# Every second chunk of the up-projections by seven products of halves, and the gated products by way of DRAM

## The chip, the cores and the metric

The kernel runs on one core of one Trainium2 chip. The time is the device time of one launch in microseconds (us), the median of several runs. The engines of the core run side by side, each through its own list of instructions in order, and wait for each other by semaphores: TensorE (PE in the profile, its weight loads PEld), VectorE (DVE), ScalarE (ACT), GpSimd (POOL) and the queue that issues the transfers (SP). TensorE writes its results into eight banks of accumulator memory (PSUM), each 128 partitions by 512 float32; all other tiles lie in on-chip memory (SBUF), 128 partitions wide.

## The reference

A trunk of two decoder layers over a residual stream of 512 tokens by 1024 features, float32. Layer 0 mixes by dilated banded attention, layer 1 by forgetting attention over shared keys and values; after each mixer stands a gated ConvFFN, and it is the ConvFFN that the change touches:

```python
def conv_ffn(xn, w_up, cw, cb, w_down):
    a = xn @ w_up                                   # (512, 1024) @ (1024, 5632)
    T = a.shape[1]
    ap = jnp.pad(a, ((0, 0), (CONV_W - 1, 0), (0, 0)))
    a = sum(ap[:, j:j + T] * cw[j] for j in range(CONV_W)) + cb
    gate, val = jnp.split(a, 2, axis=-1)            # 2816 gates, 2816 values
    return (jax.nn.gelu(gate, approximate=True) * val) @ w_down
```

After it the result is normed and added to the stream. Between the two layers a shared key, value and forget-gate projection is computed from the stream.

## The kernel before

**Products.** Every float32 operand is kept as two tiles, a rounded high part (type fp32r) and the rest. `mm3` (L228) makes one float32 product of three matmuls: high by high (L229), high by low (L230), low by high (L231).

**Weights.** All weight matrices are one list of pieces in the order of use. `Weights` loads a piece (one slab, 128 x 1024 float32, 512 KB; L41, on SP's queue, into a tile `wraw` of the pool t4), `high` rounds it on ScalarE (L49), `low` subtracts on VectorE (L55), and both go into one tile `w` of the pool t8. `get` (L64) hands out the next piece and first splits pieces until `ahead - 1` more are ready; loads go `ahead_dma` pieces further. The order of all instructions on every engine is that of the program text: nothing is reordered, and an instruction that waits holds up all behind it on its engine.

**The ConvFFN** (`ffn`, L497). The activations stand transposed as `bd.xT`: four tiles of the pool t8 (two high, two low), each 128 features by 4 groups by 512 tokens. The 2816 gates and values are 22 chunks of 128 each. For chunk c a product of 24 matmuls with 512 columns gives the gates in one bank, and another the values (`up`; `feat_mm`, L307); the first two chunks are computed in halves of 256 tokens (`first_products`, L465) because the last token blocks arrive late. After the products of chunk c comes `post(c)`: per bank one ACTIVATE on ScalarE (L517, middle tap and bias), two instructions on VectorE (L518, L520, the other taps), then the GELU on ScalarE (L522) and the gated product on GpSimd (L525), which is kept in six tiles `hT` of the pool t8. The down-projection (`Proj`, L315) takes the 22 pieces of `w_down` as moving operands and the gated products, split in pairs of chunks by `prep` (L505 ScalarE, L506 VectorE), as weights, into eight banks `acc`. Its last four pieces are worked block by block, and `Boundary` norms each block (L236 to L283) and transposes it for the next stage.

**After the first ConvFFN** four token blocks of shared values are computed from four pieces (`values`, from L905). Blocks 2 and 3 are transposed in the middle of that (`bd2.transpose`), and `W.ahead` there is 4, and 3 from the transpose of block 2 on (L921).

**Pools.** t8 has 17 tiles of 8 KB a partition, t4 9 of 4 KB, t2 6 of 2 KB; a tile handed out again waits until its last user is done.

## Time and profile before

| | |
|---|---|
| median of 3 runs | 1169.48 us (1168.93 to 1169.65) |
| the profiled execution | 1168.88 us, span 1167.1 us |
| TensorE busy | 1153.6 us, 99% of the span |
| VectorE, ScalarE, GpSimd busy | 57%, 44%, 17% |
| the two stretches of `up` products (chunks 2 to 21 of a layer) | 217.6 and 217.7 us |
| transfers | 115.72 MB, mean 99 GB/s |

The span is what lies between the first and the last instruction of the profiled execution; its own time lies 1.8 us above it. A row of the timeline gives start, duration, engine, line, operation, the tile written and the tiles read, and in brackets how long the engine stood idle before and what released it. Matmuls are pipelined: a row's duration overlaps the next matmul, so the pace is read from the starts. "x2" in a row says that two instructions in a row were merged; the duration is that from the start of the first to the end of the last.

### The profile page before, as it was taken

What the parts mean: (1) busy time and instruction counts of PE and PEld (TensorE: products, weight loads), DVE (VectorE), ACT (ScalarE), POOL (GpSimd) and SP (SyncE); (2) the same over time, 40 slices, a digit from 0 to 9 for tenths busy, and PEclk for the clock granted to TensorE, in tenths of its full rate; (3) what the DMA queues carried; (4) which work ended last, traced back from release to release, by engine and by line L of the source; (5) the groups of instructions that cost most, each with busy time, mean ns of one, the idle gap of its engine ahead of it and who ended that gap; (6) DMA issues with size and microseconds to landing.
All of it is one profiled execution on the core that took longest, in us unless ns stands there. A gap on an engine that the chain in (4) does not pass through costs nothing.

```text
span 1167.1 us, 15131 instructions
## 1 busy us (share of the span) xinstructions
PE 1153.6 (99%) x5898; PEld 960.1 (82%) x5898; DVE 663.8 (57%) x991; ACT 515.8 (44%) x900; POOL 203.9 (17%) x231
## 2 busy tenths in 40 slices
PE   9999999999999999999999999999999999999997
PEld 6888889888888888888778888789888888888886
DVE  6433586655655674406464788757566566575304
ACT  5444665333433463306462677755433334354202
POOL 2722000212212210000000565400122122120000
PEclk9999999999999999999999999999999999999999
DMA  8131063333333355203204344264332332244001
GB/s 294 53 110 37 3 182 109 103 97 108 90 91 108 93 167 169 60 1 85 81 1 128 100 119 126 76 201 126 91 109 83 99 108 88 93 145 162 1 1 72
DMA packets 134849, 115.72 MB, mean 99 GB/s; under 512 B 5753, under 2 KB 119913, under 8 KB 134778
## 3 DMA queue, kind: packets, MB, share of 16 engines
q1 hardware_dynamic: 133498, 110.57, 31.0%
q0 software_dynamic: 1280, 4.20, 1.5%
q8 instruction: 46, 0.75, 0.3%
q14 instruction: 25, 0.20, 0.1%
HBM read 108.41 MB, written 2.15 MB: 95 GB/s over the span
## 4 chain that ended last, share of the span: by engine, by line
PE 89%; DVE 5%; ACT 3%; issue 2%; DVEq 0%; ACTq 0%
PE up L231 12%; PE up L229 12%; PE up L230 12%; PE acc L229 9%; PE acc L230 9%; PE acc L231 9%; PE v_ps L229 2%; PE v_ps L231 2%; PE v_ps L230 2%; PE qk_ps L230 2%; PE qk_ps L229 2%; PE qk_ps L231 2%; PE first L229 1%; PE first L230 1%; PE first L231 1%
## 5 line engine op out<-in xcount | busy, mean ns | idle before, releaser
L55 DVE TENSOR_TENSOR w<-wraw,w 128x1024 fp32r<-128x1024 f32 x182 | 262.3, 1467 | 93.5 <-ACT w L49 93.0
L49 ACT CAST w<-wraw 128x1024 fp32r<-128x1024 f32 x182 | 184.9, 1048 | 61.6 <-PE acc L231 38.3
L517 ACT ACTIVATE bb<-up,conv 128x512 f32<-128x512 f32 x80 | 62.4, 780 | 272.8 <-PE up L231 272.8
L525 POOL TENSOR_TENSOR hT<-bb 128x512 f32<-128x512 f32 x44 | 92.8, 2108 | 490.8 <-DVE bb L520 348.9
L518 DVE SCALAR_TENSOR_TENSOR bb<-up,conv,bb 128x511 f32<-128x511 f32 x80 | 60.0, 749 | 173.0 <-ACT bb L517 173.0
L229 PE MATMUL acc<-w,hs 128*128 128x512 f32 (+1 forms) x356 | 138.0, 388 | 1.1 <-DVE mix L276 1.1
L230 PE MATMUL acc<-w,hs 128*128 128x512 f32 (+1 forms) x356 | 137.8, 387 | 0.0
L231 PE MATMUL acc<-w,hs 128*128 128x512 f32 (+1 forms) x356 | 137.8, 387 | 0.0
L229 PE MATMUL up<-xbh,w 128*128 128x512 f32 x320 | 124.6, 389 | 0.0
L230 PE MATMUL up<-xcl,w 128*128 128x512 f32 x320 | 124.6, 389 | 0.0
L231 PE MATMUL up<-xbh,w 128*128 128x512 f32 x320 | 124.6, 389 | 0.0
L230 PE MATMUL up<-xbl,w 128*128 128x512 f32 x320 | 124.6, 389 | 0.0
L229 PE MATMUL up<-xch,w 128*128 128x512 f32 x320 | 124.6, 389 | 0.0
L231 PE MATMUL up<-xch,w 128*128 128x512 f32 x320 | 124.6, 389 | 0.0
L229 PEld LDWEIGHTS acc<-w,hs 128*128 128x128 f32 x356 | 66.9, 188 | 14.9 <-DVE mix L276 1.3
L231 PEld LDWEIGHTS acc<-w,hs 128*128 128x128 f32 x356 | 66.9, 188 | 13.5
L230 PEld LDWEIGHTS acc<-w,hs 128*128 128x128 f32 x356 | 66.9, 188 | 13.5
L231 PEld LDWEIGHTS up<-xch,w 128*128 128x128 f32 x320 | 60.1, 188 | 12.6
L229 PEld LDWEIGHTS up<-xbh,w 128*128 128x128 f32 x320 | 60.1, 188 | 12.5
L230 PEld LDWEIGHTS up<-xbl,w 128*128 128x128 f32 x320 | 60.1, 188 | 12.5
L230 PEld LDWEIGHTS up<-xcl,w 128*128 128x128 f32 x320 | 60.1, 188 | 12.5
L231 PEld LDWEIGHTS up<-xbh,w 128*128 128x128 f32 x320 | 60.1, 188 | 12.3
(241 smaller groups left out, 2085.7 us busy)
## 6 DMA issues: line engine op xcount, KB each, us to landing
wraw<-in_w_up_dram SPq DMA_DIRECT2D x88, 512.0 KB
wraw<-in_w_down_dram SPq DMA_DIRECT2D x44, 512.0 KB
wraw<-in_w_kvf_dram SPq DMA_DIRECT2D x16, 512.0 KB
wraw<-in_w_qkv_a_dram SPq DMA_DIRECT2D x16, 256.0 KB
wraw<-in_w_q_b_dram SPq DMA_DIRECT2D x8, 512.0 KB
ck<-cd SPq DMA_DIRECT2D x8, 512.0 KB
qst<-qst POOLq DMA_DIRECT2D x16, 256.0 KB, 3.5
wraw<-in_w_o_b_dram SPq DMA_DIRECT2D x8, 512.0 KB
```

The source lines that it names most:

```text
L49: self.nc.scalar.copy(pair[:, 0], raw)
L55: self.nc.vector.tensor_tensor(pair[:, 1], raw, pair[:, 0].bitcast(F32), ALU.subtract)
L229: pe.matmul(o, ah, bh, start=first, stop=False, skip_group_check=shared)
L230: pe.matmul(o, ah, bl, start=False, stop=False, skip_group_check=shared)
L231: pe.matmul(o, al, bh, start=False, stop=last, skip_group_check=shared)
L517: act.activation(bb[:, s, :], ps, AF.Identity, bias=cp[:, 3, ch:ch + 1], scale=cp[:, 2, ch:ch + 1])
L518: dve.scalar_tensor_tensor(bb[:, s, 1:], ps[:, :T - 1], cp[:, 1, ch:ch + 1], bb[:, s, 1:], ALU.mult, ALU.add)
L525: pool.tensor_tensor(hT[c // 4][:, c % 4, :], bb[:, 0, :], bb[:, 1, :], ALU.mult)
```

## The change

**Seven products.** For the chunks in `SEVEN` (6, 8, ... 20, eight in each layer) gates and values are taken as one product of a 2 x 2 matrix of weight halves (gates over values, first over second half of the 1024 input features) by a 2 x 2 matrix of activation halves (first over second half of the features, first and second 256 tokens). It is computed by seven products of such halves and sums in place of eight: each product is 12 matmuls with 256 columns. The sums of activations (`sums_in`: two additions on GpSimd, four subtractions on VectorE, then high and low parts in four new tiles XA and XB) are made once per layer during chunks 2 to 5. The sums of weights (`seven_weights`) are made for every such chunk two chunks ahead: four subtractions or additions of 512 columns on VectorE, and four pairs of high and low parts in place of two. The partial results are combined in the banks: a copy on ScalarE (`s1`) and five additions on VectorE, some of them between products that go on accumulating in the same bank. Between them stand the steps of the weights for chunk c + 2 and, before the last product, the first half of the gates of chunk c + 1 (`begun`).

**The chunk's end.** `post` of a chunk is put behind the first products of the next one. The gated product moves from GpSimd to VectorE, one chunk later still; it goes into a t2 tile `hc` and from there by a transfer of 256 KB to a DRAM tensor `hD`. For the down-projection `prep` reads two chunks at a time (512 KB) back into t4 tiles `hraw`. The six tiles `hT` are gone.

**Weights.** During `ffn` `W.ahead` is 1, and the steps of splitting are placed by hand between products; before the down-projection it is 4 again. In the values after the first ConvFFN it is 1 until block 3 is transposed, and then one piece is split per block.

```diff
--- before.py
+++ after.py
@@ -55,6 +55,13 @@
             self.nc.vector.tensor_tensor(pair[:, 1], raw, pair[:, 0].bitcast(F32), ALU.subtract)
             self.ready[self.n_split] = (pair[:, 0], pair[:, 1])
             self.n_split += 1
+    def take(self, k):
+        self.load(self.n_split + k + self.ahead_dma)
+        raws = [self.raw.pop(self.n_split + i) for i in range(k)]
+        self.n_split += k
+        return raws
 
     def split(self, n):
         while self.n_split < min(n, len(self.pieces)):
@@ -494,14 +501,25 @@
         dve.tensor_copy(cp, pc)
         return cp
 
+    SEVEN = range(6, NF - 1, 2)
     def ffn(bd, cp, nxt, ahead):
-        hT = [None] * 6
-        hs = {}
+        hD = tc.dram_tile([NF, 128, T], F32, name="hD")
+        hraw, hs, hc = {}, {}, {}
+        def load_h(j):
+            if j < NF // 2:
+                hraw[j] = t4([128, 2, T], name="hraw")
+                sp.dma_start(hraw[j], hD[2 * j:2 * j + 2].rearrange("c p t -> p c t"))
 
         def prep(j):
             if j < NF // 2:
+                load_h(j + 1)
                 hs[j] = t = t8([128, 2, 2, T], F32R, name="hs")
-                src = hT[j // 2][:, 2 * (j % 2):2 * (j % 2) + 2, :]
+                src = hraw.pop(j)
                 act.copy(t[:, 0], src)
                 dve.tensor_tensor(t[:, 1], src, t[:, 0].bitcast(F32), ALU.subtract)
 
@@ -510,7 +528,7 @@
                 prep(kc // 2 + 1)
             return hs[kc // 2][:, 0, kc % 2], hs[kc // 2][:, 1, kc % 2]
 
-        def post(c, banks):
+        def taps(c, banks):
             bb = t4([128, 2, T], name="bb")
             for s, ch in ((0, c), (1, NF + c)):
                 ps = banks[s]
@@ -519,25 +537,173 @@
                                          ALU.mult, ALU.add)
                 dve.scalar_tensor_tensor(bb[:, s, 2:], ps[:, :T - 2], cp[:, 0, ch:ch + 1], bb[:, s, 2:],
                                          ALU.mult, ALU.add)
+            return bb
+        gated = []
+        def product():
+            if gated:
+                c, bb = gated.pop()
+                if c - 1 in hc:
+                    sp.dma_start(hD[c - 1], hc.pop(c - 1))
+                hc[c] = t2([128, T], name="hc")
+                dve.tensor_tensor(hc[c], bb[:, 0, :], bb[:, 1, :], ALU.mult)
+        def glu(c, bb):
             act.activation(bb[:, 0, :], bb[:, 0, :], AF.Gelu_apprx_tanh)
-            if c % 4 == 0:
-                hT[c // 4] = t8([128, 4, T], name=f"hT{c // 4}")
-            pool.tensor_tensor(hT[c // 4][:, c % 4, :], bb[:, 0, :], bb[:, 1, :], ALU.mult)
-
+            gated.append((c, bb))
+        def post(c, banks):
+            product()
+            glu(c, taps(c, banks))
+        xT = None
+        XA, XB = [], []
+        def sums_in():
+            v = [t8([128, 4, T], name=f"xsum{i}") for i in range(2)]
+            for i in range(2):
+                pool.tensor_tensor(v[i], xT[0][i].bitcast(F32), xT[1][i].bitcast(F32), ALU.add)
+            yield
+            dve.tensor_tensor(v[0][:, :, LO], v[0][:, :, HI], v[0][:, :, LO], ALU.subtract)
+            dve.tensor_tensor(v[0][:, :, HI], v[1][:, :, HI], v[0][:, :, HI], ALU.subtract)
+            yield
+            dve.tensor_tensor(v[1][:, :, HI], v[1][:, :, HI], v[0][:, :, LO], ALU.subtract)
+            dve.tensor_tensor(v[1][:, :, LO], v[1][:, :, LO], v[1][:, :, HI], ALU.subtract)
+            yield
+            for X, src in ((XA, v[0]), (XB, v[1])):
+                X += [t8([128, 4, T], F32R, name="xsh"), t8([128, 4, T], F32R, name="xsl")]
+                for k in (0, 2):
+                    act.copy(X[0][:, k:k + 2], src[:, k:k + 2])
+                    dve.tensor_tensor(X[1][:, k:k + 2], src[:, k:k + 2], X[0][:, k:k + 2].bitcast(F32), ALU.subtract)
+                    yield
+        halves = {}
+        def split_pair(pair, src, n=1024):
+            act.copy(pair[:, 0, :n], src)
+            yield
+            dve.tensor_tensor(pair[:, 1, :n], src, pair[:, 0, :n].bitcast(F32), ALU.subtract)
+        def seven_weights(c):
+            r0, r1 = W.take(2)
+            w = [t8([128, 2, 1024], F32R, name="w") for _ in range(4)]
+            sa, sb = (t4([128, 1024], name="wsum") for _ in range(2))
+            a11, a12, a21, a22 = r0[:, 0:512], r0[:, 512:1024], r1[:, 0:512], r1[:, 512:1024]
+            act.copy(w[0][:, 0], r0)
+            dve.tensor_tensor(sa[:, 0:512], a11, a21, ALU.subtract)
+            dve.tensor_tensor(sb[:, 0:512], a21, a22, ALU.add)
+            yield
+            dve.tensor_tensor(sa[:, 512:1024], sb[:, 0:512], a11, ALU.subtract)
+            act.copy(w[1][:, 0], sa)
+            dve.tensor_tensor(sb[:, 512:1024], a12, sa[:, 512:1024], ALU.subtract)
+            yield
+            dve.tensor_tensor(w[1][:, 1], sa, w[1][:, 0].bitcast(F32), ALU.subtract)
+            act.copy(w[2][:, 0], sb)
+            yield
+            dve.tensor_tensor(w[0][:, 1], r0, w[0][:, 0].bitcast(F32), ALU.subtract)
+            act.copy(w[3][:, 0, 0:512], a22)
+            yield
+            dve.tensor_tensor(w[2][:, 1], sb, w[2][:, 0].bitcast(F32), ALU.subtract)
+            yield
+            dve.tensor_tensor(w[3][:, 1, 0:512], a22, w[3][:, 0, 0:512].bitcast(F32), ALU.subtract)
+            v = [t.rearrange("p s (q k c) -> p s q k c", q=2, k=4) for t in w]
+            halves[c] = dict(A11=v[0][:, :, 0], A12=v[0][:, :, 1], S3=v[1][:, :, 0], S2=v[1][:, :, 1],
+                             S1=v[2][:, :, 0], S4=v[2][:, :, 1], A22=v[3][:, :, 0])
+        def plain_weights():
+            for _ in range(2):
+                W.high()
+                W.low()
+                yield
+        def weights(c):
+            return seven_weights(c) if c in SEVEN else plain_weights()
+        def half_mm(o, w, x, s, start):
+            for k in range(4):
+                mm3(o, w[:, 0, k, :], w[:, 1, k, :], x[0][:, k, s], x[1][:, k, s], start and k == 0, k == 3, True)
+        def up(w, o, kcs):
+            wh, wl = (t.rearrange("p (k c) -> p k c", k=8) for t in w)
+            for kc in kcs:
+                bh, bl = xs(xT, kc, ALL)
+                mm3(o, wh[:, kc, :], wl[:, kc, :], bh, bl, kc == 0, kc == KD - 1)
+        base = W.n_get
         first = first_products(bd, 4)
+        xT = bd.xT
         post(0, first[0:2])
         post(1, first[2:4])
+        W.ahead = 1
+        W.split(base + 8)
+        extra = sums_in()
+        begun = None
+        before = None
         for c in range(2, NF):
+            if c == NF - 2:
+                load_h(0)
             if c == NF - 1:
                 prep(0)
                 prep(1)
-            banks = []
-            for s in range(2):
-                o = bank([128, T], name="up")
-                feat_mm(W.get(), bd.xT, o, ALL)
-                banks.append(o)
-            post(c, banks)
-
+            steps = weights(c + 2)
+            banks = [bank([128, T], name="up") for _ in range(2)]
+            if c in SEVEN:
+                w = halves.pop(c)
+                W.n_get += 2
+                x11, x21, x22 = [(xT[0][i], xT[1][i], s) for i, s in ((0, LO), (1, LO), (1, HI))]
+                o1, o2, o3, o4 = banks[0][:, LO], banks[0][:, HI], banks[1][:, LO], banks[1][:, HI]
+                s1, s12, s17 = (t2([128, 256], name="csum") for _ in range(3))
+                def prod(o, a, x, start=False):
+                    half_mm(o, w[a], x[0:2], x[2], start)
+                prod(o1, "A11", x11, True)
+                prod(o2, "S2", (*XB, HI))
+                prod(o3, "S3", (*XA, HI), True)
+                product()
+                bb = taps(*before)
+                act.copy(s1, o1)
+                next(steps)
+                dve.tensor_tensor(s12, o2, s1, ALU.add)
+                dve.tensor_tensor(s17, o3, s1, ALU.add)
+                glu(before[0], bb)
+                prod(o1, "A12", x21)
+                prod(o2, "S1", (*XA, LO))
+                prod(o3, "A22", (*XB, LO))
+                next(steps)
+                next(steps, None)
+                dve.tensor_tensor(o4, o2, s17, ALU.add)
+                begun = W.get(), bank([128, T], name="up")
+                up(*begun, range(4))
+                prod(o2, "S4", x22)
+                next(steps, None)
+                dve.tensor_tensor(o3, o3, s12, ALU.add)
+                next(steps, None)
+                dve.tensor_tensor(o2, o2, s1, ALU.add)
+            else:
+                for s in range(2):
+                    if s == 0 and begun:
+                        w, banks[0] = begun
+                        up(*begun, range(4, KD))
+                        begun = None
+                    else:
+                        up(W.get(), banks[s], range(KD))
+                    if s == 0 and before:
+                        post(*before)
+                    next(steps, None)
+                    next(extra, None)
+            for _ in steps:
+                pass
+            before = c, banks
+        post(*before)
+        product()
+        sp.dma_start(hD[NF - 1], hc.pop(NF - 1))
+        W.ahead = 4
         Proj(NF, 4, get_act).finish(nxt, ahead)
 
 
@@ -910,6 +1076,7 @@
     bd2.norm(3)
     banks = [bank([128, 512], name="v_ps") for _ in range(4)]
     wv = []
+    W.ahead = 1
     for sp_, blocks in ((0, (0, 1)), (2, (0, 1)), (0, (2,)), (2, (2,)), (0, (3,)), (2, (3,))):
         if len(wv) < 4:
             wv += [value_weight(), value_weight()]
@@ -918,9 +1085,11 @@
                 values(banks, wv[s], s, (b,))
             if (sp_, b) == (2, 0):
                 bd2.transpose(2)
-                W.ahead = 3
         if (sp_, blocks) == (0, (2,)):
             bd2.transpose(3)
+            W.ahead = 3
+        if blocks[0] > 1:
+            W.split(min(W.n_split + 1, W.n_get + W.ahead))
         if sp_ == 2 and blocks[-1] > 1:
             for bb in (blocks[0] - 2, blocks[0]):
                 keep_values(0, bb, banks[bb])
```

## The prediction

> **What bounds the kernel now.** I read the page first, then the stretches, then the starts of the matmuls, and last the rows of the other engines.
>
> ```profile
> PE 1153.6 (99%) x5898; PEld 960.1 (82%) x5898; DVE 663.8 (57%) x991; ACT 515.8 (44%) x900; POOL 203.9 (17%) x231
> PEclk9999999999999999999999999999999999999999
> PE 89%; DVE 5%; ACT 3%; issue 2%; DVEq 0%; ACTq 0%
> ```
>
> TensorE is busy throughout, at a granted clock in the top tenth, and makes up 89% of the chain that ended last. So the matmuls count, provided that no other engine becomes late. The two stretches of `up`, by the windows:
>
> ```profile
> 205.40:423.00 217.60, 217.60 (x962) 180.29 (x961) 129.73 (x122) 81.25 (x102) 42.94 (x20) 1.00 0.34 100
> 822.20:1039.90 217.70, 217.70 (x963) 180.41 (x962) 129.74 (x122) 81.22 (x102) 42.90 (x20) 1.00 0.34 100
> ```
>
> After the length stand the busy times of PE, PEld, DVE, ACT and POOL: TensorE has no gap, VectorE works 129.7 of 217.6 us. The pace is in the starts, 42 matmuls of 256 columns apart, then 45 of 512:
>
> ```profile
> 185.02 0.28 PE L231 MATMUL first<-xbh,w 128*128 128x256 f32 x1
> 190.06 0.28 PE L231 MATMUL first<-xbh,w 128*128 128x256 f32 x1
> ...
> 206.60 0.39 PE L231 MATMUL up<-xbh,w 128*128 128x512 f32 x1
> 216.80 0.39 PE L231 MATMUL up<-xbh,w 128*128 128x512 f32 x1
> ```
>
> 5.04/42 = 0.1200 us and 10.20/45 = 0.2267 us. Half the columns cost 53% of the time.
>
> **The matmuls.** A plain chunk is 48 x 0.2267 = 10.88 us; a chunk of seven products is 7 x 12 x 0.1200 = 10.08 us. That saves 0.80 us, 16 times: 12.8 us, far less than the eighth that the arithmetic saves. The saving would be gone at 10.88/84 = 0.1295 us a matmul. The Trainium skill (TensorE: Matmul & The Clock Gate, Back-to-back issue gap) gives N/2.4 + 2.5 ns, 109 and 216 ns; by it the saving would be an estimated 1.19 us a chunk, 19 us in all. The measured pace decides, and I keep 0.80.
>
> **Can the others keep up?** A pair (a seven-product chunk and a plain one) takes TensorE 20.96 us. The rows for the price of VectorE's and ScalarE's work:
>
> ```profile
> 347.92 0.75 DVE L518 SCALAR_TENSOR_TENSOR bb<-up,conv,bb 128x511 f32<-128x511 f32 x1 [3.84 <-ACT bb L517]
> 348.70 0.75 DVE L520 SCALAR_TENSOR_TENSOR bb<-up,conv,bb 128x510 f32<-128x510 f32 x1
> 349.38 3.45 DVE L55 TENSOR_TENSOR w<-wraw,w 128x1024 fp32r<-128x1024 f32 x2
> 349.59 2.16 POOL L525 TENSOR_TENSOR hT<-bb 128x512 f32<-128x512 f32 x1 [8.72 <-DVE bb L520]
> ...
> 188.20 2.35 DVE L55 TENSOR_TENSOR w<-wraw,w 128x1024 fp32r<-128x1024 f32 x2
> L55 DVE TENSOR_TENSOR w<-wraw,w x182: 1149/1226/2326, 37.6 to 1103.5; 128x1024 fp32r<-128x1024 f32 x182
> 178.65 1.28 DVE L301 TENSOR_TENSOR xbl<-xt_ps,xbh 128x512 fp32r<-128x512 f32 x2
> ...
> 347.10 0.78 ACT L517 ACTIVATE bb<-up,conv 128x512 f32<-128x512 f32 x1 [4.60 <-PE up L231]
> 347.78 0.62 ACT L522 ACTIVATE bb<-bb 128x512 f32<-128x512 f32 x1
> 348.30 1.99 ACT L49 CAST w<-wraw 128x1024 fp32r<-128x1024 f32 x2
> ```
>
> Two subtractions take 2.35 us alone and 3.45 us beside GpSimd's gated product. With that product gone from GpSimd I take 1.13 us each (2.35 less one full 1.22). A 512-column one starts 0.60 us after the one before (1.28 for two, 0.68 each), the two taps of a bank take 0.78 + 0.68 = 1.46 us. A 256-column one is taken from the last bank of the kernel:
>
> ```profile
> 1158.23 0.28 PE L231 MATMUL acc<-w,hs 128*128 128x256 f32 x1
> 1158.54 0.38 ACT L269 ACTIVATE junk<-acc 128x256 bf16<-128x256 f32 x1 [0.74 <-PE acc L231]
> 1159.13 0.42 DVE L276 TENSOR_TENSOR mix<-acc,gain 128x256 f32<-128x256 f32 x1
> 1159.60 0.39 PE L229 MATMUL acc<-w,hs 128*128 128x256 f32 x1 [1.09 <-DVE mix L276]
> ```
>
> 0.42 us, and 0.34 to the next. VectorE's pair is then 5 wide subtractions (5.65), 7 of 512 (four weight sums, half a low part, two gated products: 4.2), eight taps in four banks (5.84), 5 additions in the banks (1.8): 17.5 of 20.96 us, 83%. ScalarE has 5.5 casts (5.4), four ACTIVATEs (2.8), two GELUs (1.1) and the copy: 9.7 us. Neither is the bound by its sum; the order decides.
>
> The last four rows show the wait that matters. The second half of that bank is written by other matmuls than those that VectorE reads, and TensorE still waited 1.09 us: accesses to one bank follow one another, whatever their columns. In a seven-product chunk the fourth product (A12, into `o1`) therefore waits not only for the copy `s1` but for the addition `s12`, which reads `o2` in the same bank; and queued behind A12 is all of TensorE. Counted from the start of the last matmul of the previous seven-product chunk, VectorE's way to `s12` is: 0.33 (0.31 to the engine behind in the rows above, rounded up) + addition to `o2` 0.34 + half a low part 0.60 + gated product 0.60 + four taps 2.92 + 0.26 waiting for ScalarE's cast behind the GELU + two low parts 2.26 + gated product 0.60 + four taps 2.92 + two weight sums 1.20 + `s12` 0.42 = 12.45 us. TensorE's is 0.12 + 36 x 0.2267 + 36 x 0.1200 = 12.60 us. They are level, 0.15 us apart. Bounds for the stall: 0 if the paces hold; 0.5 us if each VectorE instruction costs its full duration (0.42, 0.69, 0.75, 1.22) with nothing overlapped, 13.1 us. I take 0.1, nearer to the rows of two in a row, which do overlap: each pair then saves 0.70 us, 11.2 us in all. The later waits (A22 for `s17`, S4 for `o4`) have over a microsecond: 2.72 us of `begun` lie between.
>
> **The round trip and the queue.** Each layer adds 22 stores of 256 KB and 11 loads of 512 KB on SP's queue, 23 MB in all. A store waits for a gated product, and the loads of slabs are behind it; the store belongs to a product one chunk older, so SP can still run about a chunk ahead.
>
> ```profile
> 307.11 2.60 SPq L41 DMA_DIRECT2D wraw<-in_w_up_dram  x2
> 308.10:313.40 5.30, 5.30 (x25) 4.37 (x25) 2.71 (x3) 0.78 (x1) 0.13 (x1) 1.00 0.69 201
> ACT w L49 <- DMA wraw<-in_w_up_dram: 6.1, 8, 1.0
> ```
>
> Two slabs go from issue to landed in 6.3 us (1 MB at 201 GB/s), and ScalarE has waited for such slabs only 8 times, 6.1 us in all. By my count of t4 tiles (a gain, four slabs, two weight sums, one `bb`: 8 of 9 live at most) the slabs are issued some 15 us before use. The loads of `hraw` are due a pair of chunks (10.9 us) ahead. I cost both at nothing; the cover is that distance.
>
> **The ends of `ffn`.** The activation sums fall in chunks 2 to 5. VectorE has there four times taps, gated product and low parts (4 x 5.78), eight instructions of 1024 columns for the sums (9.0) and 4.1 us more for the first seven-product weights, 36.2 of 43.5 us: 0. After chunk 21 the down-projection needs the seventh of eight banks 18 x 0.2267 = 4.1 us after its start, and VectorE frees the first bank of chunk 21 only behind `prep` and the taps of chunk 20. From the last matmul of chunk 20: 0.67 + 2.26 + 0.60 + 2.92 + 2.26 + 0.60 + 1.46 = 10.8 us, 2.5 us after the up-products end (8.3). Covered; if VectorE came another 4 us late there, waiting for `hraw`, it would cost 2.5 us a layer. I take 0.3.
>
> **The values after layer 0.** Here the removed steps are on the path:
>
> ```profile
> 552.68 2.94 ACT L49 CAST w<-wraw 128x1024 fp32r<-128x1024 f32 x3
> 553.35 1.03 PE L424 MATMUL xt_ps<-ident,xn 128*128 128x128 f32 x8
> 553.75 3.50 DVE L55 TENSOR_TENSOR w<-wraw,w 128x1024 fp32r<-128x1024 f32 x3
> 557.16 1.28 DVE L426 TENSOR_TENSOR xf<-xt_ps,gcol 128x512 f32<-128x512 f32 x2
> 556.74 0.39 PE L231 MATMUL v_ps<-w,xkl 128*128 128x512 f32 x1
> 558.55 0.50 PE L229 MATMUL v_ps<-w,xkh 128*128 128x512 f32 x1 [1.42 <-ACT xkh L431]
> ```
>
> Three splits (`ahead` 4) stand on VectorE before block 2's transposed tiles can be read, and TensorE has a gap of 558.55 - 556.74 - 0.23 = 1.58 us. With `ahead` 1 they come after block 3's transpose: `xf` then starts when the transposes end (554.4), the matmul could follow 1.39 us later as it does now (558.55 - 557.16), at 555.8, and is due at 556.97. Saved: 1.6 us, bounds 0 and 1.6; block 2's low part is late next.
>
> **Sum** against the profiled execution: 1168.88 - 11.2 - 1.6 + 0.6 = 1156.7 us. The median of the runs stands 0.6 us above that execution: 1157.3 us, 1.0% faster.
>
> **Rivals.**
> (1) VectorE a little late. With full durations the stall is 0.5 us a pair: 16 x 0.3 + 1.6 = 6.4 us saved, about 1163 us; for it speaks the margin of only 0.15 us, against it the overlapping rows. The Trainium skill (VectorE: DVE Perf Modes, The DRAIN you can't avoid) says that the next instruction starts only when the pipe is empty, which is this rival; the trace's 2.35 us for two of 1.22 us does not quite agree.
> (2) Slower: the slabs of the next chunk land late. The first step of the weights (two sums over both slabs) stands on VectorE ahead of `s12`, so a late slab holds all of TensorE at A12. If the loads are issued only after the last low part of the plain chunk (7.3 us after the count's start), they land at 13.6 us, `s12` is done at 15.3, and the stall is 2.7 us: 16 x 1.9 more, about 1198 us. It turns the sign once `s12` comes 0.9 us late. For it: SP's stores in front of the loads; against it: the small waits for slabs now.
> (3) No change: the seven-product matmuls run at 0.1295 us or more, because each weight load now follows another 0.12 us later and products switch tiles and banks. Then only the values' 1.6 us are left, 1168 us. Against it: `first` runs at 0.1200 with the same shapes.
>
> **The numbers.** A change of 0.2%, 2.3 us, is about what a measurement of this kernel can tell from none. The forecast, 1155 to 1160.5 us: 0.62. Rival 1, 1160.5 to 1167: 0.16. Rival 3 and other ways within 0.2%: 0.05. Rival 2 and others of its kind: 0.17. Faster 0.78, same 0.05, slower 0.17. The range goes down to 1154.5 us (no stall at all: 12.8 + 1.6 saved, 1155.1 by the median) and up to 1170 us, which leaves out rival 2.
>
> **What the profile after would show.** Products of 256 columns starting 0.120 us apart; a pair from one A11 to the next in 20.9 to 21.2 us; DVE about 83% busy in these stretches, its wide subtractions at 1.15 to 1.23 us; TensorE waiting, if at all, at the fourth product for `s12`; the gap at the values gone. Waits of ScalarE or VectorE for `wraw`, or of the first `acc` products for a bank, would make the forecast wrong.

## The result and the profile after

The changed kernel takes 1158.71 us (median of 5 runs, 1158.16 to 1159.27); the kernel before took 1169.11 us beside it (5 runs, 1168.69 to 1169.65). The ratio is 0.9909, with a 95% interval of 0.9898 to 0.9920: 0.9% faster. The forecast was 1157.3 us. The span of the profiled execution went from 1167.1 to 1156.9 us.

From the page of the changed kernel, the busy times and the shares of the chain that ended last:

```profile
PE 1142.1 (99%) x6474; PEld 977.5 (84%) x6474; DVE 767.1 (66%) x1227; ACT 554.9 (48%) x956; POOL 131.5 (11%) x191
PE 90%; DVE 4%; ACT 3%; issue 2%; DVEq 0%; ACTq 0%
```

TensorE issues 576 matmuls more and is busy 11.5 us less. It is still the bound. VectorE is busy 103 us more, and the chain still passes through it for only 4%.

The first layer's stretch of `up` in the windows of the changed kernel, from the first matmul into `up` to the first into `acc`, and below it one steady pair (the second layer's stretch is 213.48 us). After the length stand PE, PEld, DVE, ACT and POOL, then granted clock, DMA share and GB/s:

```profile
205.62:419.08 213.46, 211.80 (x1251) 188.78 (x1249) 174.98 (x236) 100.69 (x131) 0.00 (x0) 1.00 0.42 125
364.10:385.10 21.00, 21.00 (x134) 19.08 (x133) 17.72 (x26) 9.79 (x13) 0.00 (x0) 1.00 0.44 127
```

Each layer's stretch is 4.2 us shorter (it was 217.6), 8.3 us together; the rest of the 10.2 us lies between the two stretches, where the gap at the values was. In the pair TensorE never stops. VectorE has 17.72 of 21.0 us (the prediction said 17.5), ScalarE 9.79 (9.7). But over the whole stretch TensorE lacks 1.66 us of the length, and that is one place. First the place where nothing is lost, chunk 18, in the timeline (start, duration, engine, line, operation):

```profile
378.94 0.42 DVE L671 TENSOR_TENSOR csum<-up,csum 128x256 f32<-128x256 f32 x1
379.38 0.29 PE L238 MATMUL up<-xsh,w 128*128 128x256 f32 x1
379.51 0.29 PE L236 MATMUL up<-xbh,w 128*128 128x256 f32 x1
```

L671 is `s12`. It ends at 379.36, and the fourth product (A12, the first `xbh` row) starts at 379.51, 0.13 us behind the matmul before it: on time, by 0.15 us. The same place in chunk 20:

```profile
399.53 1.05 ACT L49 CAST w<-wraw 128x1024 fp32r<-128x1024 f32 x1
400.38 0.28 PE L238 MATMUL up<-xsh,w 128*128 128x256 f32 x1
400.62 1.23 DVE L55 TENSOR_TENSOR w<-wraw,w 128x1024 fp32r<-128x1024 f32 x1 [1.79 <-ACT w L49]
401.76 0.42 DVE L671 TENSOR_TENSOR csum<-up,csum 128x256 f32<-128x256 f32 x1
402.32 0.36 PE L236 MATMUL up<-xbh,w 128*128 128x256 f32 x1 [1.66 <-DVE csum L671]
```

Here VectorE sits idle for 1.79 us, waiting for a cast of ScalarE's, then does a low part, and only then `s12`. TensorE's gap is 402.32 - 400.38 = 1.94 us, of which 0.12 is the ordinary distance: 1.82 us lost, once in each layer. In the changed kernel's waits this is the only entry in which TensorE waits in the up-projections (total, times, longest, in us), and the waits for DMAs beside it are small:

```profile
PE up L236 <- DVE csum L671: 3.3, 2, 1.7
...
ACT w L49 <- DMA wraw<-in_w_up_dram: 5.9, 8, 0.8
ACT hs L523 <- DMA hraw<-hD: 4.1, 10, 1.6
```

The slabs of the up-projection are waited for as often as before (8 times), and the loads of the gated products 10 times, all on ScalarE. TensorE has no wait behind them in these stretches.

The values after layer 0, from the changed kernel's timeline:

```profile
550.00 1.29 DVE L433 TENSOR_TENSOR xf<-xt_ps,gcol 128x512 f32<-128x512 f32 x2 [0.23 <-PE xt_ps L431]
...
552.76 0.39 PE L238 MATMUL v_ps<-w,xkl 128*128 128x512 f32 x1
552.99 0.39 PE L236 MATMUL v_ps<-w,xkh 128*128 128x512 f32 x1
```

`xf` no longer stands behind three low parts, and block 2's first `xkh` matmul follows at the ordinary 0.23 us.

### The profile page after: what moved, and what is told of

The parts are those of the page before. It is cut to its first block, busy times and chain, and to the rows that moved or that the text cites. A ratio compares the mean times of both kernels' runs of the same rounds, so it can differ in the third digit from the quotient of the medians.

```text
span 1156.9 us, 16648 instructions
## 1 busy us (share of the span) xinstructions
PE 1142.1 (99%) x6474; PEld 977.5 (84%) x6474; DVE 767.1 (66%) x1227; ACT 554.9 (48%) x956; POOL 131.5 (11%) x191
## 4 chain that ended last, share of the span: by engine, by line
PE 90%; DVE 4%; ACT 3%; issue 2%; DVEq 0%; ACTq 0%
PE up L236 12%; PE up L237 12%; PE up L238 12%; PE acc L236 9%; PE acc L238 9%; PE acc L237 9%; PE v_ps L236 2%; PE v_ps L238 2%; PE v_ps L237 2%; PE qk_ps L237 2%; PE qk_ps L236 2%; PE qk_ps L238 2%; PE first L238 1%; PE first L236 1%; PE first L237 1%
## 5 line engine op out<-in xcount | busy, mean ns | idle before, releaser
L55 DVE TENSOR_TENSOR w<-wraw,w 128x1024 fp32r<-128x1024 f32 x150 | 189.6, 1279 | 119.2 <-ACT w L49 117.4
L49 ACT CAST w<-wraw 128x1024 fp32r<-128x1024 f32 x150 | 154.2, 1049 | 81.4 <-PE acc L238 56.0
L236 PE MATMUL up<-xch,w 128*128 128x512 f32 (+1 forms) x288 | 102.2, 355 | 1.7 <-DVE csum L671 1.7
L236 PE MATMUL up<-xbh,w 128*128 128x512 f32 (+1 forms) x288 | 102.1, 355 | 1.7 <-DVE csum L671 1.7
L237 PE MATMUL up<-xcl,w 128*128 128x512 f32 (+1 forms) x288 | 102.0, 354 | 0.0
L237 PE MATMUL up<-xbl,w 128*128 128x512 f32 (+1 forms) x288 | 102.0, 354 | 0.0
L238 PE MATMUL up<-xch,w 128*128 128x512 f32 (+1 forms) x288 | 101.8, 354 | 0.0
L238 PE MATMUL up<-xbh,w 128*128 128x512 f32 (+1 forms) x288 | 101.8, 354 | 0.0
L236 PEld LDWEIGHTS acc<-w,hs 128*128 128x128 f32 x356 | 66.8, 188 | 14.8 <-DVE mix L283 1.3
L236 PE MATMUL up<-xsh,w 128*128 128x256 f32 x256 | 72.4, 283 | 0.0
L237 PE MATMUL up<-xsl,w 128*128 128x256 f32 x256 | 72.4, 283 | 0.0
L238 PE MATMUL up<-xsh,w 128*128 128x256 f32 x256 | 72.4, 283 | 0.0
L276 ACT ACTIVATE junk<-acc 128x512 bf16<-128x512 f32 (+1 forms) x33 | 19.2, 582 | 92.4 <-PE acc L238 92.1
L236 PEld LDWEIGHTS up<-xbh,w 128*128 128x128 f32 x288 | 54.4, 189 | 9.5 <-ACT w L49 1.8
```

The lines of the kernel that those rows point to most:

```text
L49: self.nc.scalar.copy(pair[:, 0], raw)
L55: self.nc.vector.tensor_tensor(pair[:, 1], raw, pair[:, 0].bitcast(F32), ALU.subtract)
L236: pe.matmul(o, ah, bh, start=first, stop=False, skip_group_check=shared)
L237: pe.matmul(o, ah, bl, start=False, stop=False, skip_group_check=shared)
L238: pe.matmul(o, al, bh, start=False, stop=last, skip_group_check=shared)
L276: act.activation(junk[:, :s.stop - s.start], o, AF.Square, scale=1.0 / 32, accum_out=ss[:, n % 2:n % 2 + 1])
```

## The experiments

Theory A: the change is worth its matmuls, and what is missing of that is decided by what VectorE has in its queue ahead of `s12`; the round trip through DRAM and the mere amount of VectorE's work cost nothing. Against it stand, one by one, the amount of VectorE's work, the end of the stretch (where the reads of the gated products begin), the round trip, and contention with GpSimd. Medians are compared with the 1158.71 us of the changed kernel; ratios are to the kernel before in the same session (1169.1 to 1169.3 us).

**1. Chunk 20's weights behind the sums.** In chunk 20 the weights in preparation are plain ones, so its first step is a cast and a low part that waits for it. Only there, the step is moved behind `s12` and `s17`:

```
-                next(steps)
+                if c + 2 in SEVEN:
+                    next(steps)
                 dve.tensor_tensor(s12, o2, s1, ALU.add)
                 dve.tensor_tensor(s17, o3, s1, ALU.add)
+                if c + 2 not in SEVEN:
+                    next(steps)
```

> The changed kernel with one edit: in chunk 20, where the weights two chunks on are plain pieces of the down-projection, the step of their splitting (a cast on ScalarE, then a subtraction on VectorE that waits for it) is put behind the additions s12 and s17 instead of ahead of them. Theory A (the fourth product waits for s12, and s12 for that cast and subtraction; the gap of 1.94 us against 0.12 in each layer is this alone): both gaps go, 2 x 1.8 us, 1155.1 us against 1158.7. Rival B (the gap at chunk 20 comes from the reads of the DRAM tensor that begin there, or from late slabs): the gap stays, 1158.7 us.

Measured: 1154.97 us (1154.94 to 1155.15), ratio 0.9877 [0.9863, 0.9892]. The window of the first stretch of `up`, and rows of its timeline at a change from 256 to 512 columns:

```profile
205.68:417.26 211.58, 211.58 (x1251) 188.73 (x1250) 175.08 (x236) 100.69 (x131) 0.00 (x0) 1.00 0.42 126
```

```profile
367.07 0.40 PE L236 MATMUL up<-xbh,w 128*128 128x512 f32 x1
...
367.77 0.40 PE L236 MATMUL up<-xbh,w 128*128 128x512 f32 x1
```

TensorE's busy time now equals the length of the stretch (and of the second, 211.56 us): no matmul waits. So 3.7 us of the changed kernel hung on one statement's place in one chunk. Without any stall a stretch is 217.6 - 211.6 = 6.0 us shorter than before, where eight chunks of 0.80 us make 6.4. The other 0.4 us a layer lies in the 512-column matmuls: the first three distances after the change of width take 367.77 - 367.07 = 0.70 us, 0.233 each, where 0.2267 was the pace. There are two such changes in a pair, 16 in a layer, and 16 x 0.02 us are 0.3.

**2. The seven-product chunks end at 18.** If the end of the stretch, with its reads of the gated products, were at fault, chunk 18 in the last place should not show the same gap at the same statement.

```
-    SEVEN = range(6, NF - 1, 2)
+    SEVEN = range(6, NF - 3, 2)
```

> The changed kernel with seven products in chunks 6 to 18 only, seven chunks a layer instead of eight. Theory A: the chunk whose successor's weights are plain pieces is now 18, so the gap of 1.9 us moves there, and one saving of 0.80 us a layer less the cost of two changes of width is lost: 1160.2 us. Rival B (the gap belongs to chunk 20, to the reads of the DRAM tensor): no gap at 18, 1156.6 us.

Measured: 1160.26 us, ratio 0.9924 [0.9909, 0.9939]. Chunk 18, which had no stall, in this kernel's timeline:

```profile
379.54 0.28 PE L238 MATMUL up<-xsh,w 128*128 128x256 f32 x1
379.76 1.23 DVE L55 TENSOR_TENSOR w<-wraw,w 128x1024 fp32r<-128x1024 f32 x1 [1.79 <-ACT w L49]
381.47 0.36 PE L236 MATMUL up<-xbh,w 128*128 128x256 f32 x1 [1.66 <-DVE csum L671]
```

The gap is the same 1.93 us and has moved with the last seven-product chunk, whose successor's weights are plain; the 1.5 us more are the 0.8 us that a chunk saves, twice. So it is neither chunk 20 nor the distance to the down-projection. That it is the step of the plain weights, and not the last place in the row of seven-product chunks as such, follows from the first experiment, where the last chunk keeps its place and the gap goes.

**3. No seven-product chunk.** Eight products everywhere, with the gated products still on VectorE and by way of DRAM, and the values as changed:

```
-    SEVEN = range(6, NF - 1, 2)
+    SEVEN = range(0)
...
-        extra = sums_in()
+        extra = iter(())
```

> The changed kernel without seven products and without the sums of activations: every chunk by eight products; the later post, the gated product on VectorE, the way by DRAM and the order of splitting stay. Theory A (all that is left of the gain is the gap at the values, 1.6 us, and the round trip costs nothing): 1167.5 us, TensorE without a gap in the up stretches (217.6 us each). Rival B (the round trip or the later post costs, hidden in the sum): 1169 us or more, with gaps at the start of the down-projection.

Measured: 1167.15 us (10 runs), ratio 0.9981 [0.9972, 0.9991]. One stretch in its windows:

```profile
206.01:423.64 217.63, 217.63 (x962) 180.25 (x961) 121.00 (x143) 82.23 (x103) 0.00 (x0) 1.00 0.42 123
```

The stretch is as long as before and without a gap, so stores, loads, and the product on VectorE cost nothing here, where VectorE is busy 121 us of the stretch. That they cost nothing beside its 175 us either is shown by the stretch of the first experiment, in which TensorE never waits. What this kernel still gains, about 2 us, is what the next experiment takes away.

**4. The values as before.** Only the order of the splits at the values is undone:

```
-    W.ahead = 1
...
+                W.ahead = 3
...
-            W.ahead = 3
-        if blocks[0] > 1:
-            W.split(min(W.n_split + 1, W.n_get + W.ahead))
```

> The changed kernel with the old splitting in the values after layer 0 (ahead 4, and 3 from the transpose of block 2 on). Theory A: the gap of 1.6 us at the third token block comes back, 1160.3 us. Rival B (the gap went because tiles come free earlier now that hT is gone): no gap, 1158.7 us.

Measured: 1160.93 us, ratio 0.9928 [0.9913, 0.9943], 2.2 us above the changed kernel. In its timeline the gap is back, 1.82 us with the ordinary distance in it:

```profile
552.72 0.39 PE L238 MATMUL v_ps<-w,xkl 128*128 128x512 f32 x1
554.54 0.50 PE L236 MATMUL v_ps<-w,xkh 128*128 128x512 f32 x1 [1.43 <-ACT xkh L438]
```

**5 and 6. One sum more, two sums more, ahead of `s12`.** The margin of 0.15 us is tested by making one of the weight sums of each seven-product chunk a second time (and, in the sixth, a third) in the same tile:

```
             dve.tensor_tensor(sa[:, 0:512], a11, a21, ALU.subtract)
+            dve.tensor_tensor(sa[:, 0:512], a11, a21, ALU.subtract)
             dve.tensor_tensor(sb[:, 0:512], a21, a22, ALU.add)
```

> The changed kernel with one weight sum of 512 columns (0.60 us on VectorE) made twice, ahead of s12, in every chunk that makes seven-product weights. Theory A (the fourth product waits for s12 because both use one bank; in the trace s12 ends 0.15 us before the product is due): a stall of 0.45 to 0.6 us in chunks 8 to 18 of each layer, 12 times, a little in chunk 6: 5.5 to 8 us more, about 1165 us. Rival B (only the fifth product, which writes the columns that s12 reads, has to wait): it is due 1.44 us later, so nothing, 1158.7 us. Rival C (only VectorE's sum counts, 18.1 of 21 us a pair): nothing.

> As before with the sum made three times: 1.20 us more ahead of s12. Theory A: 1.05 to 1.2 us in 12 chunks and some in chunk 6: 13 to 16 us more, about 1173 us, slower than the kernel before the change. Rival B (the fifth product waits): margin 1.6 us, nothing, 1158.7 us. Rival C (VectorE's sum, 18.7 of 21 us): nothing.

Measured: 1168.87 us (10 runs), ratio 0.9997 [0.9988, 1.0006], with one sum; 1180.23 us, ratio 1.0094 [1.0077, 1.0111], with two. In the timeline of the fifth kernel, VectorE and TensorE at one of the seven-product chunks:

```profile
316.64 0.68 DVE L597 TENSOR_TENSOR wsum<-wraw 128x512 f32<-128x512 f32 x1
317.36 0.69 DVE L598 TENSOR_TENSOR wsum<-wraw 128x512 f32<-128x512 f32 x1
317.97 0.69 DVE L599 TENSOR_TENSOR wsum<-wraw 128x512 f32<-128x512 f32 x1
318.57 0.42 DVE L672 TENSOR_TENSOR csum<-up,csum 128x256 f32<-128x256 f32 x1
```

```profile
318.28 0.28 PE L238 MATMUL up<-xsh,w 128*128 128x256 f32 x1
319.04 0.38 PE L236 MATMUL up<-xbh,w 128*128 128x256 f32 x1 [0.48 <-DVE csum L672]
319.26 0.28 PE L237 MATMUL up<-xbl,w 128*128 128x256 f32 x1
```

The wait for `s12` in the waits of the fifth and of the sixth kernel:

```profile
PE up L236 <- DVE csum L672: 9.9, 16, 1.7
```

```profile
PE up L236 <- DVE csum L673: 21.4, 16, 1.8
```

All sixteen seven-product chunks now wait. The margin can be read off: the repeated sum pushes the next by 317.36 - 316.64 = 0.72 us; A12 starts 0.05 us after the end of `s12` (318.99), so of the 0.15 us about 0.1 were free; 0.72 - 0.10 = 0.62, and the stall is 319.04 - 318.28 - 0.12 = 0.64 us. In chunk 6 of each layer it is 0.55 us; twelve of the one and two of the other are 8.8 us. The other 1.4 us come from the start after the stall: the second matmul follows the first by 0.22 us in place of 0.12, fourteen times. Both kernels cost more than expected (10.2 and 21.5 us), because the expectations had the repeated sum at 0.60 us, twelve chunks and little of chunk 6, and no price for the start. With a single 0.7 us instruction more in the wrong place the whole gain is gone, with two the kernel is slower than before the change.

**7. Two sums more, behind `s12`.** The same two repeated sums, with the first step of the seven-product weights moved behind `s12` and `s17` (and chunk 20 as in the changed kernel):

```
-                next(steps)
+                if c + 2 not in SEVEN:
+                    next(steps)
                 dve.tensor_tensor(s12, o2, s1, ALU.add)
                 dve.tensor_tensor(s17, o3, s1, ALU.add)
+                if c + 2 in SEVEN:
+                    next(steps)
```

> The same 1.20 us of extra sums, but the whole first step of the weights stands behind s12 and s17 instead of ahead of them. Theory A (the place on VectorE's list decides, not the sum): s12 then ends 1.2 us sooner in its chunk than in the changed kernel, no stall, 1158.7 us within 1. Rival C (VectorE is the bound by its sum): as slow as with the sums ahead, about 1173 us.

Measured: 1158.54 us, ratio 0.9906 [0.9891, 0.9920]. The same additional work that cost 21.5 us ahead of `s12` costs nothing behind it. In its timeline, `s12` (L674 here) waits for the copy `s1` and not for VectorE's own queue:

```profile
378.41 0.42 DVE L674 TENSOR_TENSOR csum<-up,csum 128x256 f32<-128x256 f32 x1 [0.35 <-ACT csum L671]
```

**8. The gated product on GpSimd again.** It was there before the change; the trip through DRAM stays.

```
-                dve.tensor_tensor(hc[c], bb[:, 0, :], bb[:, 1, :], ALU.mult)
+                pool.tensor_tensor(hc[c], bb[:, 0, :], bb[:, 1, :], ALU.mult)
```

> The changed kernel with the gated product back on GpSimd, all else as it is. Theory A (two gated products of 0.60 us leave VectorE's way to s12; GpSimd starts as soon as the GELU is done, mostly beside taps, which read one operand from the banks): s12 is not later, 1158.7 us within 1, though some subtractions show 1.5 to 2.3 us. Rival B (GpSimd slows VectorE's subtractions as in the kernel before, 1.1 us each, at two places of the pair): s12 up to 1 us late, 8 to 13 us more.

Measured: 1173.47 us, ratio 1.0036 [1.0023, 1.0049], 14.8 us above the changed kernel. It is the slowest version that does only the needed work. Theory A had expected no loss, and rival B 8 to 13 us: rival B is right in kind and too low. One stretch and one microsecond behind the longest stall in its windows, then the wait for `s12` in its waits, then VectorE and GpSimd in the timeline at three places:

```profile
205.45:426.27 220.82, 215.04 (x1250) 190.62 (x1249) 188.37 (x216) 101.37 (x131) 38.61 (x22) 0.99 0.40 121
259.40:260.40 1.00, 1.00 (x7) 1.00 (x6) 0.96 (x1) 1.00 (x3) 0.00 (x0) 0.50 0.13 38
```

```profile
PE up L236 <- DVE csum L671: 11.4, 4, 4.0
```

```profile
203.95 10.18 POOL L568 TENSOR_TENSOR xsum<-xbh,xbl 128x2048 f32<-128x2048 f32 x2
207.93 9.52 DVE L55 TENSOR_TENSOR w<-wraw,w 128x1024 fp32r<-128x1024 f32 x3
...
255.03 1.49 POOL L551 TENSOR_TENSOR hc<-bb 128x512 f32<-128x512 f32 x1 [6.47 <-DVE bb L538]
255.31 1.75 DVE L598 TENSOR_TENSOR wsum<-wraw 128x512 f32<-128x512 f32 x1
257.46 0.39 PE L236 MATMUL up<-xbh,w 128*128 128x256 f32 x1 [3.99 <-DVE csum L671]
...
378.57 1.29 POOL L551 TENSOR_TENSOR hc<-bb 128x512 f32<-128x512 f32 x1 [11.08 <-DMA wraw<-in_w_up_dram]
378.60 3.49 DVE L55 TENSOR_TENSOR w<-wraw,w 128x1024 fp32r<-128x1024 f32 x2 [0.26 <-ACT w L49]
```

VectorE has 20 instructions fewer in the stretch and is busy 13.4 us longer. The weight sum that takes 0.68 us takes 1.75 beside GpSimd's product, the pair of subtractions 3.49 in place of 2.36: 1.07 and 1.13 us more, though one has half the columns of the other. What was left of GpSimd's instruction at their start was 255.03 + 1.49 - 255.31 = 1.21 and 378.57 + 1.29 - 378.60 = 1.26 us; the delay is that, less 0.13 or 0.14. So, as far as the rows tell, VectorE's instruction does not run slower but waits until GpSimd's is over. The Trainium skill (SBUF — State Buffer, SBUF: two separate sides) says just that: the two engines share a pair of ports, an instruction of VectorE's with two SBUF inputs and GpSimd's exclude each other for the whole instruction. The trace agrees.

Where the 14.8 us go can be read from the rows. The largest part is not the gated product's own time but an order on GpSimd. The two additions of activation sums (10.18 us) now stand behind the gated product of chunk 0 in GpSimd's list and start at 203.95; in the changed kernel they are over before VectorE's low parts begin:

```profile
192.38 10.19 POOL L568 TENSOR_TENSOR xsum<-xbh,xbl 128x2048 f32<-128x2048 f32 x2 [52.38 <-DVE xbl L308]
208.09 3.50 DVE L55 TENSOR_TENSOR w<-wraw,w 128x1024 fp32r<-128x1024 f32 x3
```

Three low parts of VectorE take 9.52 us beside them in place of 3.50. VectorE does not make that up before chunk 6, where TensorE stands still for 4.15 us in the first layer (4.13 in the second). Then something comes in that no expectation had: behind this stall the granted clock is 0.50 for about 3 us, as the second window shows, and the 256-column matmuls start 0.213 us apart in place of 0.120. That costs another 1.5 us a layer. The stalls of up to 1.9 us in the other runs are not followed by it. In chunks 8 to 18 TensorE waits 0.17 us each time and loses 0.10 at the start behind it, 1.6 us a layer. Together that is 4.1 + 1.6 (clock and start) + 1.6 = 7.3 us, and the stretch is 220.82 - 213.46 = 7.36 us longer. A kernel with the additions ahead of that first gated product was not run.

**9. The first step behind the sums in all seven-product chunks.**

```
-                next(steps)
                 dve.tensor_tensor(s12, o2, s1, ALU.add)
                 dve.tensor_tensor(s17, o3, s1, ALU.add)
+                next(steps)
```

> The changed kernel with the first step of the weights behind s12 and s17 in every seven-product chunk, chunk 20 included. Theory A (the gaps of chunk 20 are the only stall, and TensorE's pace is the bound elsewhere): like the version with chunk 20 alone reordered, 1155.0 us; the margin of 0.15 us before the fourth product grows by about 1.2 us without bringing time. Rival (small stalls elsewhere in the pair cost some of the saving): up to 1 us less than that.

Measured: 1154.95 us (1154.9 to 1155.73), ratio 0.9881 [0.9867, 0.9896]: the same as the first experiment. One stretch in its windows:

```profile
206.46:418.01 211.55, 211.55 (x1250) 188.73 (x1249) 175.68 (x236) 100.69 (x131) 0.00 (x0) 1.00 0.43 126
```

There is no stall (the second layer's stretch is 211.55 us too), and the kernel no longer depends on 0.15 us: `s12` ends 0.41 us before A12 in every seven-product chunk.

**10. As 9, with the gated product on GpSimd.** The edits of 8 and 9 together.

> The same, with the gated product back on GpSimd. If GpSimd costs time only by what it adds on VectorE ahead of s12 (each VectorE instruction with two SBUF operands beside it takes 1.1 us longer, whatever its width), the steady pairs have no stall any more, and only chunk 6, for which VectorE was 4.1 us late with GpSimd, keeps about 1.8 us in each layer: 1158 to 1159 us. If GpSimd's products slow the pair by VectorE's sum or by held tiles, some 10 us more, 1165 us or above.

Measured: 1159.34 us, ratio 0.9918 [0.9903, 0.9933], a little above the expected range. Of the 14.8 us of the eighth experiment 4.4 are left. The two stretches are 1.9 us longer each than in the ninth, and that is one stall in each layer, in chunk 6 (in this kernel `s12` is L670); the other 0.5 us of the profiled execution lie behind the second stretch, and their cause was not looked for:

```profile
254.89 0.42 DVE L670 TENSOR_TENSOR csum<-up,csum 128x256 f32<-128x256 f32 x1
255.36 0.39 PE L236 MATMUL up<-xbh,w 128*128 128x256 f32 x1 [1.69 <-DVE csum L670]
```

From chunk 8 on `s12` is in time in spite of GpSimd. So contention costs time where it falls on the way to `s12`. For chunk 6 the rows point again to the three low parts beside the additions of activations, 9.51 us in this kernel's timeline. Chunk 6 is not short of time by itself: in the ninth kernel `s12` waits there 0.93 us for the copy `s1`.

**11. As 9, with seven products from chunk 4 on.** One more chunk a layer would save 0.8 us; the activation sums are then squeezed into chunks 2 and 3.

```
-    SEVEN = range(6, NF - 1, 2)
+    SEVEN = range(4, NF - 1, 2)
...
                     next(extra, None)
+                    if c < 4:
+                        next(extra, None)
```

> Sums first, and seven products from chunk 4 on, nine chunks a layer; the activation sums are made in chunks 2 and 3. TensorE alone would save 2 x 0.74 us more, 1153.5 us. VectorE's work up to chunk 4's fourth product is by the rows about 26 us where 23 us are there, so a stall of up to 3 us a layer at chunk 4 is likely: 1154 to 1160 us, no better than sums first with eight chunks.

Measured: 1160.57 us, ratio 0.9927 [0.9911, 0.9944], 5.6 us slower than the ninth and just above the expected range. From its timeline, chunk 4:

```profile
230.01 0.28 PE L236 MATMUL up<-xsh,w 128*128 128x256 f32 x1
231.58 0.39 PE L237 MATMUL up<-xsl,w 128*128 128x256 f32 x1 [1.29 <-DVE xsl L580]
...
233.60 0.28 PE L238 MATMUL up<-xsh,w 128*128 128x256 f32 x1
235.40 0.39 PE L236 MATMUL up<-xbh,w 128*128 128x256 f32 x1 [1.52 <-DVE csum L670]
```

Here the amount counts: VectorE has not finished the activation sums when the second product needs them, then is late with `s12`. Two gaps of 1.57 and 1.80 us a layer are more than the chunk saves.

## Why the prediction came out right, point by point

The forecast was 1157.3 us and the time is 1158.71; on the profiled execution 12.2 us were forecast as saved, and 10.2 were. The mechanism held: TensorE's matmuls set the time, and the one wait that costs is the one named, the fourth product's for `s12`. That the difference is so small is partly luck, because errors cancel: 2.2 us were set aside for a stall in every pair and for the ends of `ffn`, which did not come, and 4.4 us in chunk 20 and at the changes of width were not foreseen.

- **The matmuls** (0.80 us a chunk): right in kind. The 256-column distance is 0.120 us, as read from `first`. The 512-column one is (211.55 - 672 x 0.120)/576 = 0.2273 us on the mean of the ninth experiment's stretch, in place of 0.2267. A chunk without stalls saves 12.1/16 = 0.76 us. The prediction had no price for changing the width; by the first experiment it costs 16 x 0.80 - 12.1 = 0.7 us in all. The formula that the prediction quotes from the Trainium skill (TensorE: Matmul & The Clock Gate, Back-to-back issue gap) is given there for an isolated matmul, not for a stream of weight loads and matmuls like this one; the prediction rightly kept to the measured pace.
- **The sums of the other engines**: right, 17.72 and 9.79 us against 17.5 and 9.7.
- **The way to `s12`**: the margin of 0.15 us was right to the hundredth (379.36 against 379.51). This is no accident of the sum: counted as the prediction counts, from the start of the last matmul of chunk 16 at 366.88, `s12` ends after 12.48 us and A12 starts after 12.63, where 12.45 and 12.60 were forecast. That TensorE stops there if VectorE is later was shown by the fifth and sixth experiments, where fourteen chunks that had not waited did. The stall of 0.1 us a pair taken on top of it was wrong by its whole size: there is none, 1.6 us too much. What can be used of the margin is less than the prediction had it, about 0.1 us, since 0.05 pass between the end of `s12` and A12.
- **Same-bank accesses follow one another**: the wait for `s12` is there, and A12 writes other columns than `s12` reads. That the first product into the bank waits, and not only the fifth, which writes the columns that `s12` reads, was shown by the fifth experiment. Why the bank is the unit was not tested. The Trainium skill (PSUM — Partial Sum Buffer, PSUM bank collisions raise a hardware error) says that the chip does not hold back the second access and that the program has to keep engines apart by bank; by that the wait is a semaphore of the program's, which is how the waits list it, and not a property of the bank.
- **The step that failed**, though the forecast as a whole held, is the count over sixteen like chunks ("each pair then saves 0.70 us, 11.2 us in all"). Chunk 20 is unlike the others: the weights prepared in it are plain ones, since chunk 20 is the last with seven products, and their first step is a cast on ScalarE and a low part that waits for it, ahead of `s12`, where the others have two sums of VectorE's that wait for nobody. It costs 3.7 us by the first experiment. It could be read from the code: the statement is the same, but what it yields differs.
- **The round trip and SP's queue** at nothing: right by the third experiment, with 217.63 us a stretch. Rival 2, slabs that land late, did not come about.
- **The ends of `ffn`** at 0.6 us: nothing was found. The first `acc` follows the last `up` at the ordinary distance in the changed kernel's timeline:

```profile
1029.64 0.39 PE L238 MATMUL up<-xch,w 128*128 128x512 f32 x1
1029.87 0.39 PE L236 MATMUL acc<-w,hs 128*128 128x512 f32 x1
```

- **The values** at 1.6 us: right, somewhat small; the fourth experiment gives 2.2. The gap itself is 1.6 us in its rows too (1.82 less 0.23). Another 0.4 us lies in the next three matmuls there, the second of which waits for block 2's low part; the prediction named that wait and gave it no price.
- **Rival 1**, each VectorE instruction at its full duration: `s12` would have been 0.5 us late in every pair. Two subtractions of 1.22 us take 2.36 in a row in the changed kernel too, and no pair before chunk 20 shows a stall. The section of the Trainium skill that the prediction names for this rival (VectorE: DVE Perf Modes, The DRAIN you can't avoid) itself adds that a next instruction that is not held starts earlier, and the 2.36 us agree with that. It was the nearest rival in time but not in mechanism. **Rival 3**: the pace is 0.120 us and not 0.1295.

The terms together: 12.8 - 0.7 (width) - 3.7 (chunk 20) + 2.2 (values) = 10.6 us, where the medians differ by 10.4.

## What to carry to other kernels

A shared statement in a loop that draws from a generator stands for different work in the iterations at the edges: go through the first and the last one by hand, above all for an instruction that waits for another engine and stands ahead of one that TensorE needs. When two engines run level, put the short instruction that the bound waits for at the head of its engine's queue and the preparation behind it; here that was worth 3.7 us, made extra sums free that cost 21.5 us in front, and widened a margin of 0.15 us to 0.41. Before moving work to another engine, look also at what already stands in that engine's list: the product put on GpSimd pushed 10 us of additions into VectorE's way. Fewer operations by a cleverer algorithm save only what the pace of the smaller pieces leaves: an eighth of the products gave 7% of a chunk's time.

## What the runs showed that was not expected

- In the rows shown, a GpSimd product of 1.29 to 1.49 us adds 1.07 to 1.13 us to the VectorE instruction with two SBUF inputs that starts beside it, the narrow as well as the wide one: GpSimd's remaining time less 0.13 or 0.14. Moving a product from VectorE (0.68 us) to GpSimd therefore made VectorE busier, 188.4 against 175.0 us a stretch, 6.0 us of it by the additions that stand behind the product.
- After a stall of 4.1 us TensorE's granted clock was 0.50 for about 3 us; after stalls of up to 1.9 us the matmuls kept their pace of 0.120 us from the third on.
- After a stall TensorE's second 256-column matmul follows 0.19 to 0.22 us behind the first, not 0.12, which adds about 0.1 us to each stall.
- After a change from 256 to 512 columns the first matmuls are 0.233 us apart, not 0.227. Why wasn't tried.
- A 512-column VectorE instruction that writes the same columns of a tile as the one before it starts 0.72 us after that, where one into another tile starts 0.60 or 0.61 us after.
